# Low halves of the index key made on VectorE in place of GpSimd, in a hybrid retention and sparse-attention layer

## The chip, the cores and the metric

The kernel runs on one core of one Trainium2 chip, in one launch. The metric is the device time of that core in microseconds; lower is better. Times of "before" and "after" are medians of several executions; one further execution of each is recorded by the hardware profiler, and every duration below comes from that recorded execution.

## The reference

One decoder layer on 512 tokens of width 1024, in float32. One projection feeds two groups of heads: four heads of chunked retention, and four heads of attention over 128 keys per query that an indexer selects. The rest is an output projection, a layer norm, a SwiGLU block of 2816 hidden units and a second layer norm. What the change touches is the indexer:

```python
iq = rope(iq.reshape(B, S, IDX_HEADS, IDX_DIM), positions)      # 8 index heads of 64
ik = rope(ik[:, :, None, :], positions)[:, :, 0, :]             # one index key per token
...
logits = jax.nn.relu(jnp.einsum('bqhd,bsd->bqhs', qb, kf))
score = jnp.einsum('bqh,bqhs->bqs', wb, logits)
score = jnp.where(key_pos[None, None, :] <= pb[None, :, None], score, -jnp.inf)
_, sel = lax.top_k(score, topk)
```

## The kernel before

**Precision by halves.** TensorE's fast float32 form (`float32r`) rounds its operands, so the kernel writes a value as a high half (a cast) and a low half (value minus high half), and `mm3` (L93 to L96) makes one product out of three matmuls: high by high (L94), high by low (L95 or L96), low by high. For weights, `split` (L85 to L91) makes the high half with a ScalarE cast (L86). The low half is made either by a VectorE subtraction (L91) or, for a share of the weights, by a ScalarE copy with sign reversed (L88) and a DMA from GpSimd's queue that adds the raw weight to it in memory (L89).

**The stage around the change.** The order of instructions is written out by hand; each engine runs its own list strictly in that order. `proj_feature(c)` projects 128 output features at a time: weight number k = 2c + i goes to the accumulator `pf{c}_{i}`, with 24 matmuls of 128x512 each. There are four accumulators of that tag in PSUM, used in turn. Weights 0 to 3 and every even one have their low half from VectorE; the odd ones from 5 on have it by the DMA on GpSimd's queue. When an accumulator is finished, `rope` (L229 to L238) turns it: three VectorE multiplications (L233 to L235), which read PSUM, and one GpSimd addition (L237), which reads two SBUF tiles. Raw weights come in chunks of two on SyncE's queue into three buffers (`raw`). A buffer is free once its last low half is made; for weights made by the DMA that means once that DMA has landed.

**The index key and the logits.** `index_rope` (L251 to L299) runs beside the projection, a step at a time. It turns the index key into `ks` (L286, VectorE), then calls `halves_k` (L255). That casts the high half `kh` on ScalarE (L256) and makes the low half in two blocks of 32 partitions, 0 to 31 and 64 to 95 (L259). After each block two DMAs on GpSimd's queue copy low and high half into the neighbouring 32 partitions (L260, L261). In the profile `kh` and both low tiles are called `kk`. `logits(j)` (L406) multiplies the eight index heads of a block of 128 queries with them, two matmuls a head (L415, L416); ScalarE applies the relu (L417), VectorE adds the head up in `score` (L421 for head 0, L423 for the others). Below, "head 4" is the fifth of the eight heads of block 1, the first block that is computed. The PSUM tiles of these logits, called `lg`, are of the other tag, again four in turn. The tile before head 0 in that turn holds the turned head weights (`iwp`), so head 4 takes the tile of head 0 and can start only when L421 has read it.

**TensorE's list here:** the last matmuls of `pf3_0` (weight 6); head 0; nine matmuls of `pf3_1` (weight 7, the low half by DMA); heads 1 and 2; nine more of `pf3_1`; heads 3 and 4; the last six of `pf3_1`; heads 5 and 6; `pf4_0`, and so on.

Of the kernel before, what the change touches and what calls it, by code (L numbers as in the profile page):

```python
# [9 lines left out]
F32 = mybir.dt.float32  # L10
# [3 lines left out]
ALU = mybir.AluOpType  # L14
# [39 lines left out]
def hybrid_layer_kernel(ctx: ExitStack, tc: tile.TileContext, xT, x, pos, w0, wf, wt, wo,  # L54
                        wgu, wd, gng, lmg, lmb, lfg, lfb, ident_d, cols_d, masks_d, decay_d, out):
    nc = tc.nc
    V, A, G, T = nc.vector, nc.scalar, nc.gpsimd, nc.tensor
# [12 lines left out]
    def psu(name):  # L70
        return psp.tile([P, 512], F32, tag="u", name=name)

    def tmp(name, dt=F32):
        return tp.tile([P, 512], dt, tag="t", name=name)
# [154 lines left out]
    def rope(dst, src, ct, st, lo=0):  # L229
        t1 = tmp("rt1")  # L230
        t2 = tmp("rt2")
        n = slice(lo, S)
        V.tensor_tensor(t1[:, n], src[:, n], ct[:, n], op=ALU.mult)  # L233
        V.tensor_tensor(t2[0:64, n], src[64:128, n], st[64:128, n], op=ALU.mult)
        V.tensor_tensor(t2[64:128, n], src[0:64, n], st[0:64, n], op=ALU.mult)  # L235
        if dst is not None:
            G.tensor_tensor(dst, t1[:, n], t2[:, n], op=ALU.add)  # L237
        return t1, t2  # L238
# [6 lines left out]
    kh, kl = kk3[:, 0], (kk3[:, 1], kk3[:, 2])  # L245
# [5 lines left out]
    def index_rope():  # L251
        G.memset(kk3[:, 1:].bitcast(F32), 0.0)
        rounding = lambda: None

        def halves_k(ks):  # L255
            A.copy(kh, ks)  # L256
            for b in (0, 64):
                s, d = slice(b, b + 32), slice(b + 32, b + 64)
                G.tensor_tensor(kl[0][s], ks[s], kh[s].bitcast(F32), op=ALU.subtract)  # L259
                nc.gpsimd.dma_start(kl[1][d].bitcast(F32), kl[0][s].bitcast(F32))  # L260
                nc.gpsimd.dma_start(kh[d].bitcast(F32), kh[s].bitcast(F32))  # L261

        def halves_q(i, qs):
            A.copy(qa[:, i], qs[:, P:])
            A.copy(qb[:, i], qs[:, P:])
            G.tensor_tensor(ql[:, i], qs[:, P:], qa[:, i].bitcast(F32), op=ALU.subtract)
            if i % 2:
                n = slice(i - 1, i + 1)
                for d, s in ((qa[32:64, n], ql[0:32, n]), (qa[96:128, n], ql[64:96, n]),
                             (qb[0:32, n], ql[32:64, n]), (qb[64:96, n], ql[96:128, n])):  # L270
                    nc.gpsimd.dma_start(d.bitcast(F32), s.bitcast(F32))

        for i in range(4):
            t1, t2 = rope(None, acc0[1 + i], CI, SI, P)
            qs = tmp("qs")
            V.tensor_tensor(qs[:, P:], t1[:, P:], t2[:, P:], op=ALU.add)
            rounding()
            rounding = lambda i=i, qs=qs: halves_q(i, qs)
            yield 2.3
        rounding()  # L280
        while len(key) < 3:
            yield 1.0
        A.copy(iwr, acc0[0])
        t1, t2 = rope(None, acc0[0], CI, SI)
        ks = tmp("ks")
        V.tensor_tensor(ks, t1, t2, op=ALU.add)  # L286
        yield 1.7
        halves_k(ks)
        yield 5.5
        iwp = psu("iwp")  # L290
        for j in range(NB):
            T.transpose(iwp[:, j * P:(j + 1) * P], iwr[:, j * P:(j + 1) * P], ident)
        iw3 = iwp.rearrange("p (j c) -> p j c", c=P)
        A.activation(iw[:, 1:], iw3[:, 1:, 32:32 + IH], AF.Copy, scale=IDX_SCALE)
        o = 0
        for a, z in SPARE:
            A.copy(early_v[:, :, o:o + z - a], iw3[:, :, a:z])
            o += z - a
        yield 3.0  # L299
# [1363 lines left out]
```

## Time and profile before

| | before |
|---|---|
| three timed executions, us | 617.75, 618.26, 618.61 |
| their median, us | 618.26 |
| the profiled execution, us | 619.8 |
| its span (first to last instruction), us | 618.0 |
| mean granted TensorE clock in it | 0.99 |
| read from HBM / written | 74.52 MB / 2.10 MB |
| instructions on VectorE / ScalarE / GpSimd | 940 / 611 / 202 |

The profiled execution lasted 619.8 us, of which its span is 618.0; 1.8 us lie around it. It stands 1.5 us above the median of the timed ones. Instants below are counted from the start of that span.

How to read the rows: "PE" is TensorE's matmuls, "DVE" VectorE, "ACT" ScalarE, "POOL" GpSimd. A row of a timeline has start, length, engine, line, operation, output and inputs, and shapes; in square brackets is how long the engine sat idle before it, and what ended that. In the chain of waits each row is a start, a length and what the end of the kernel was waiting for then. A row of the table of stretches gives the length of the stretch, then busy time of PE, PE's weight load, DVE, ACT and POOL with instruction counts, then the granted TensorE clock (1.00 is full speed), the busy share of the DMA engines and the GB/s they moved. Numbers of tiles are left out in the profile: `pf` is any of `pf0_0` to `pf7_1`.

### The profile page before, as it was taken

The numbers are of one execution on the slowest core, as the hardware profiler recorded it, in microseconds if no ns is written. First come the engines' busy times: TensorE is split into PE (matmuls) and PEld (weight loads), VectorE is DVE, ScalarE is ACT, GpSimd is POOL, SyncE is SP. The second block draws the span as 40 slices with busy tenths as digits, with TensorE's granted clock in tenths as the row PEclk, the third lists the DMA queues.
The fourth block names the chain that finished last, engine by engine and source line by source line (L and its number), as shares of the span: only waits on it lengthen the run. The fifth ranks groups of instructions, "written<-read, shape, count | busy, mean of one in ns | idle before, by whom it ended". The sixth has DMA issues, their size and how long they took to land.

```text
span 618.0 us, 9195 instructions
## 1 busy us (share of the span) xinstructions
PE 605.4 (98%) x3256; PEld 521.5 (84%) x3256; DVE 517.7 (84%) x940; ACT 348.8 (56%) x611; POOL 186.1 (30%) x202
## 2 busy tenths in 40 slices
PE   8999899999999999999999999999999999999995
PEld 7988688888888787889998888888888988887884
DVE  6888667889888977889999989898898888977856
ACT  5443244435242557687657777777677785648300
POOL 0136612331148000233003535444343421214011
PEclk9999799999999999999999999999999999999998
DMA  8875643579663582499237888888978879689602
GB/s 277 250 233 147 170 154 103 141 167 229 180 137 102 211 335 72 136 245 179 87 136 186 180 207 168 194 197 177 207 150 188 183 213 220 155 227 293 199 34 102
DMA packets 48014, 110.77 MB, mean 179 GB/s; under 512 B 8880, under 2 KB 23280, under 8 KB 42464
## 3 DMA queue, kind: packets, MB, share of 16 engines
q1 hardware_dynamic: 25232, 77.02, 37.3%
q0 software_dynamic: 22432, 32.71, 31.8%
q8 instruction: 25, 0.41, 0.3%
q10 hardware_dynamic: 304, 0.46, 0.2%
q14 instruction: 21, 0.17, 0.1%
HBM read 74.52 MB, written 2.10 MB: 124 GB/s over the span
## 4 chain that ended last, share of the span: by engine, by line
PE 72%; issue 10%; DVE 6%; DMA 5%; POOL 4%; ACT 1%; SPq 1%; POOLq 0%; ACTq 0%; DVEq 0%
PE ga L919 10%; PE ga L921 5%; PE gc L919 5%; PE ga L927 5%; PE pf L96 3%; PE pf L94 3%; PE pf L95 3%; PE gc L921 3%; PE gb L919 3%; PE mx L96 2%; PE mx L94 2%; PE mx L95 2%; PE gc L927 2%; PE pt L95 2%; PE pt L94 2%
## 5 line engine op out<-in xcount | busy, mean ns | idle before, releaser
L86 ACT CAST wh<-raw 128x1024 fp32r<-128x1024 f32 x44 | 46.1, 1050 | 41.2 <-issue 17.5
L870 POOL DMA_DIRECT2D t<-t x34 | 29.2, 857 | 85.5 <-DVE t L1003 56.8
L96 PE MATMUL pf<-xh,wl 128*128 128x512 f32 x128 | 51.0, 399 | 2.3 <-DMA wl<-raw 2.3
L94 PE MATMUL pf<-xh,wh 128*128 128x512 f32 x128 | 51.1, 399 | 0.2 <-DVE rt L235 0.2
L95 PE MATMUL pf<-xl,wh 128*128 128x512 f32 x128 | 50.8, 397 | 0.0
L870 POOL DMA_DIRECT2D w<-w x34 | 39.2, 1194 | 32.9 <-DVE w L953 23.9
L91 DVE TENSOR_TENSOR wl<-raw,wh 128x1024 fp32r<-128x1024 f32 x26 | 32.0, 1236 | 18.0 <-ACT wh L86 17.9
L472 POOL TENSOR_TENSOR rs<-ve,half 128x1 f32<-128x1 f32 (+1 forms) x11 | 11.8, 1072 | 102.9 <-DVE ve L471 102.7
L94 PE MATMUL pt<-wh,xh 128*128 128x512 f32 (+1 forms) x96 | 38.5, 402 | 0.0
L95 PE MATMUL pt<-wl,xh 128*128 128x512 f32 (+1 forms) x96 | 37.0, 386 | 0.0
L96 PE MATMUL pt<-wh,xl 128*128 128x512 f32 (+1 forms) x96 | 36.7, 382 | 0.0
L89 POOL DMA_DIRECT2D wl<-raw x18 | 15.8, 876 | 55.3 <-ACT wl L88 55.3
L96 PEld LDWEIGHTS pf<-xh,wl 128*128 128x128 f32 x128 | 24.7, 193 | 8.0 <-DMA wl<-raw 2.7
L94 PEld LDWEIGHTS pf<-xh,wh 128*128 128x128 f32 x128 | 24.6, 192 | 5.2 <-issue 0.5
L95 PEld LDWEIGHTS pf<-xl,wh 128*128 128x128 f32 x128 | 24.6, 192 | 4.7
L417 ACT ACTIVATE lg<-lg 128x256 f32<-128x256 f32 (+2 forms) x24 | 10.9, 474 | 29.8 <-PE lg L416 29.7
L434 DVE MAX8 m<-score 128x8 f32<-128x256 f32 (+2 forms) x48 | 26.8, 558 | 1.1
L435 DVE MATCH_REPLACE8 score<-m,score 128x256 f32<-128x256 f32 (+2 forms) x48 | 26.0, 542 | 0.0
L89 POOL DMA_DIRECT2D slot<-hu x9 | 10.9, 1335 | 37.3 <-ACT slot L88 37.3
L96 PEld LDWEIGHTS pt<-wh,xl 128*128 128x128 f32 x96 | 18.0, 188 | 3.3
L94 PEld LDWEIGHTS pt<-wh,xh 128*128 128x128 f32 x96 | 18.1, 188 | 2.7
L95 PEld LDWEIGHTS pt<-wl,xh 128*128 128x128 f32 x96 | 18.1, 189 | 2.4
(1183 smaller groups left out, 1979.8 us busy)
## 6 DMA issues: line engine op xcount, KB each, us to landing
graw<-in_wgu_dram SPq DMA_DIRECT2D x22, 1024.0 KB, 5.3
wl<-raw POOLq DMA_DIRECT2D x18, 512.0 KB, 5.1
raw<-in_wo_dram SPq DMA_DIRECT2D x8, 1024.0 KB, 4.9
raw<-in_wf_dram SPq DMA_DIRECT2D x7, 1024.0 KB, 6.3
raw<-in_wt_dram SPq DMA_DIRECT2D x6, 1024.0 KB, 5.3
r<-in_wd_dram SPq DMA_DIRECT2D x12, 512.0 KB, 5.8
w<-w POOLq DMA_DIRECT2D x34, 128.0 KB, 4.1
graw<-graw POOLq DMA_DIRECT2D x17, 256.0 KB, 3.7
```

The lines of the kernel that those rows point to most:

```text
L86: A.copy(hi, src)
L89: nc.gpsimd.dma_start(lo.bitcast(F32), src, accum_op=ALU.add)
L91: eng_lo.tensor_tensor(lo, src, hi.bitcast(F32), op=ALU.subtract)
L94: T.matmul(acc, lhsT=lh, rhs=rh, start=first, stop=False, **kw)
L95: T.matmul(acc, lhsT=lh, rhs=rl, start=False, stop=False, **kw)
L96: T.matmul(acc, lhsT=ll, rhs=rh, start=False, stop=last, **kw)
L434: V.max(m8, a)
L435: V.match_replace(out=a, in_to_replace=m8, in_values=a, imm_value=TAKEN)
L870: nc.gpsimd.dma_start(t[:, :Q], t[:, Q:], accum_op=ALU.add)
L919: T.matmul(pair, lhsT=h[:, ws[k]], rhs=parts[q][:, :, k], start=first and k == 0, stop=False, skip_group_check=True)
L921: T.matmul(full[:, :Q], lhsT=l[:, ws[k]], rhs=parts[q][:, 0, k], start=False, stop=k == 3, skip_group_check=True)
L927: T.matmul(gp[n][acc], lhsT=a[:, i * S + k * P:i * S + k * P + P], rhs=parts[q][:, b, k], start=first and j == 0, stop=j == 11, skip_group ...
```

## The change

The subtraction that makes the two blocks of the key's low half is issued on VectorE in place of GpSimd. Nothing else differs: the same operands, shapes and place in the program's text.

```diff
             A.copy(kh, ks)
             for b in (0, 64):
                 s, d = slice(b, b + 32), slice(b + 32, b + 64)
-                G.tensor_tensor(kl[0][s], ks[s], kh[s].bitcast(F32), op=ALU.subtract)
+                V.tensor_tensor(kl[0][s], ks[s], kh[s].bitcast(F32), op=ALU.subtract)
                 nc.gpsimd.dma_start(kl[1][d].bitcast(F32), kl[0][s].bitcast(F32))
                 nc.gpsimd.dma_start(kh[d].bitcast(F32), kh[s].bitcast(F32))
```

On GpSimd this is the piece where it happens, between the addition of `pf1_0`'s rope and the DMA that finishes the low half of weight 7 (`wl_592`); the semaphores that each row waits for are in brackets (DMASW: an earlier DMA of GpSimd's queue, Pool: GpSimd itself).

```order
 L237 TENSOR_TENSOR akT<-rt_557,rt_558 128x512 [waits DVE_49]
-L259 TENSOR_TENSOR kk_301<-ks,kk_301 32x512 [waits Activation_49]
-L260 DMA kk_301<-kk_301 32x512 [waits DMASW4_49,Pool_49]
-L261 DMA kk_301<-kk_301 32x512 [waits DMASW5_49]
-L259 TENSOR_TENSOR kk_301<-ks,kk_301 32x512
-L260 DMA kk_301<-kk_301 32x512 [waits DMASW6_49,Pool_49]
+L260 DMA kk_301<-kk_301 32x512 [waits DMASW4_49,DVE_49]
+L261 DMA kk_301<-kk_301 32x512 [waits DMASW5_49,Activation_49]
+L260 DMA kk_301<-kk_301 32x512 [waits DMASW6_49,DVE_49]
 L261 DMA kk_301<-kk_301 32x512 [waits DMASW7_49]
 L89 DMA wl_592<-raw_358 128x1024 [waits DMAHW1_49,DMASW0_49,Activation_49]
```

GpSimd keeps its four DMAs and loses two additions of 32x512; its first and third DMA now wait for VectorE instead of for itself.

On VectorE the two subtractions land between the rope multiplications of `pf1_0` (`rt_558`) and those of `pf1_1` (`rt_600`).

```order
 L234 TENSOR_TENSOR rt_558<-pf_0_497,tables 64x512
 L235 TENSOR_TENSOR rt_558<-pf_0_497,tables 64x512
+L259 TENSOR_TENSOR kk_301<-ks,kk_301 32x512 [waits Activation_49]
+L259 TENSOR_TENSOR kk_301<-ks,kk_301 32x512
 L233 TENSOR_TENSOR rt_600<-pf_1_553,tables 128x512 [waits PE_49,Pool_49]
 L234 TENSOR_TENSOR rt_601<-pf_1_553,tables 64x512
```

All that follows on VectorE stands behind them now. That is first the rope of `pf1_1`, the low half of weight 8, the ropes of `pf2_0` and `pf2_1`, and then these rows, up to the one that reads head 0's logits (`lg_0_708`); they are the same rows in both kernels:

```order
L91 TENSOR_TENSOR wl_715<-raw_547,wh_714 128x1024
L233 TENSOR_TENSOR rt_722<-pf_0_677,tables 128x512
L234 TENSOR_TENSOR rt_723<-pf_0_677,tables 64x512
L235 TENSOR_TENSOR rt_723<-pf_0_677,tables 64x512
L421 TENSOR_SCALAR score<-lg_0_708,iw 128x256
```

TensorE's list is unchanged. Its piece with heads 3 and 4, where the wait for VectorE (DVE) is the one for the tile of head 0:

```order
L415 MATMUL lg_3_753<-kk_301,qb 128x256 [waits PE_49,Activation_49]
L416 MATMUL lg_3_753<-kk_301,qb 128x256
L415 MATMUL lg_4_758<-kk_301,qa 128x256 [waits DMASW1_49,DVE_49]
L416 MATMUL lg_4_758<-kk_301,qa 128x256
L94 MATMUL pf_1_718<-xh_76,wh_591 128x512
```

Nothing moved in it; only the instants at which what it waits for is ready can differ.

## The prediction

> **What bounds the kernel now.** I read the page first: who is busy, and what the end waited for.
>
> ```profile
> span 618.0 us, 9195 instructions
> PE 605.4 (98%) x3256; PEld 521.5 (84%) x3256; DVE 517.7 (84%) x940; ACT 348.8 (56%) x611; POOL 186.1 (30%) x202
> PE 72%; issue 10%; DVE 6%; DMA 5%; POOL 4%; ACT 1%; SPq 1%; POOLq 0%; ACTq 0%; DVEq 0%
> ```
>
> TensorE is busy nearly all the time. So what shortens this kernel is a wait of TensorE, or a stretch in which it runs slowly. The view of TensorE's waits has one wait of size in the middle of the kernel:
>
> ```profile
> PE pf L96 <- DMA wl<-raw: 2.3, 1, 2.3
> ```
>
> TensorE's timeline shows where, and what follows. Third row from the top: `pf3_1` begins, and two rows later it lacks the low half of weight 7.
>
> ```profile
> 66.90 0.39 PE L96 MATMUL pf<-xh,wl 128*128 128x512 f32 x1
> 67.42 0.36 PE L415 MATMUL lg<-kk,qa 128*128 128x256 f32 x1
> ...
> 67.74 0.40 PE L94 MATMUL pf<-xh,wh 128*128 128x512 f32 x1
> 67.97 0.39 PE L95 MATMUL pf<-xl,wh 128*128 128x512 f32 x1
> 70.66 0.80 PE L96 MATMUL pf<-xh,wl 128*128 128x512 f32 x1 [2.29 <-DMA wl<-raw]
> ...
> 77.75 0.28 PE L415 MATMUL lg<-kk,qb 128*128 128x256 f32 x1
> ...
> 77.97 0.28 PE L415 MATMUL lg<-kk,qa 128*128 128x256 f32 x1
> ```
>
> A full matmul starts 0.23 us after the one before (67.74 to 67.97), a head of block 1 takes 0.22 (77.75 to 77.97). From head 0 (67.42) to head 4 (77.97) lie 18 matmuls and four heads: 18 x 0.23 + 4 x 0.22 = 5.02 us at that pace. It took 10.55. The wait explains 2.29; the table of stretches has the rest in its clock column:
>
> ```profile
> 6.50:8.50 2.00, 1.16 (x7) 0.84 (x6) 1.25 (x2) 1.64 (x3) 0.00 (x0) 1.00 0.99 306
> ...
> 68.40:70.00 1.60, 0.00 (x0) 0.00 (x0) 0.71 (x1) 0.85 (x1) 1.60 (x2) 1.00 1.08 205
> 70.70:76.50 5.80, 5.80 (x16) 4.74 (x17) 3.31 (x6) 0.74 (x2) 2.30 (x2) 0.50 1.02 266
> 77.00:80.00 3.00, 3.00 (x18) 2.58 (x18) 0.97 (x2) 0.65 (x2) 0.00 (x0) 1.00 0.72 300
> ...
> 610.60:612.50 1.90, 0.03 (x1) 0.00 (x0) 1.79 (x5) 0.30 (x1) 0.00 (x0) 1.00 0.43 161
> 613.00:618.00 5.00, 0.00 (x0) 0.00 (x0) 1.73 (x4) 0.00 (x0) 0.00 (x0) 0.50 0.28 105
> ```
>
> After 1.6 us of idleness the granted clock halves, and it stays there until about 77. From 70.66 to 77.97 stand 16 matmuls and three heads, 4.34 us at full pace; they took 7.31, so the slow clock cost **2.97**. The idle 0.84 us between 6.5 and 8.5 (1.16 busy of 2.00) cost no clock; the idleness at the end did, after 1.9 us.
>
> Why was the low half late? The chain of waits runs back from it through GpSimd, one thing behind the other:
>
> ```profile
> 59.51 1.29 POOL akT L237
> 60.80 1.25 POOL kk L259
> ...
> 62.33 0.48 POOL kk L260
> ...
> 62.82 0.51 POOL kk L261
> ...
> 63.40 1.30 POOL kk L259
> ...
> 64.99 0.46 POOL kk L260
> ...
> 65.48 0.50 POOL kk L261
> 65.98 4.63 DMA wl<-raw
> ```
>
> The data of that DMA were there long before; here is ScalarE, then the times to landing of the `kk` DMAs and of the `wl` DMAs around here:
>
> ```profile
> 57.79 1.06 ACT L88 ACTIVATE wl<-raw 128x1024 fp32r<-128x1024 f32 x1
> ```
>
> ```profile
> DMA to landing us min/median/max: 1.8/1.9/1.9
> ```
>
> ```profile
> DMA to landing us min/median/max: 4.5/4.6/5.3
> ```
>
> So the two subtractions on GpSimd stand in a chain that ends at TensorE. They hold up head 0 a little too: the last `kk` DMA, issued at 65.48, lands at about 67.4, where head 0 starts; without that it would start at 66.90 + 0.23 = 67.13.
>
> **The change part by part.** *GpSimd* loses two operations of 1.25 and 1.30 us and the two pauses of 0.28 behind them (62.05 to 62.33, 64.70 to 64.99). The four `kk` DMAs, about 0.5 us each, could follow the addition that ends at 60.80; the `wl` DMA would be issued at 62.8 instead of 65.98 and land at 67.4 (with 5.3 at 68.1). TensorE asks for it at 67.13 + 0.22 + 2 x 0.23 = 67.81. The wait of 2.29 shrinks to 0 to 0.3, below the 0.84 that cost no clock. SyncE's next raw load, which needs this landing, starts earlier as well.
>
> *VectorE* gains the two subtractions. Their cover is an idle piece further down its list:
>
> ```profile
> 55.59 0.69 DVE L286 TENSOR_TENSOR ks<-rt,rt 128x512 f32<-128x512 f32 x1
> 56.20 1.22 DVE L91 TENSOR_TENSOR wl<-raw,wh 128x1024 fp32r<-128x1024 f32 x1
> ...
> 58.74 0.69 DVE L235 TENSOR_TENSOR rt<-pf,tables 64x512 f32<-64x512 f32 x1
> 59.45 0.69 DVE L233 TENSOR_TENSOR rt<-pf,tables 128x512 f32<-128x512 f32 x1
> ...
> 69.29 1.30 DVE L91 TENSOR_TENSOR wl<-raw,wh 128x1024 fp32r<-128x1024 f32 x1 [2.03 <-ACT wh L86]
> ...
> 72.62 0.48 DVE L421 TENSOR_SCALAR score<-lg,iw 128x256 f32<-128x256 f32 x1
> ```
>
> Nearest is L286, 512 elements from two SBUF tiles: the next row starts 0.61 later. Two are 1.22, from 59.45 on; their input, the cast `kh`, was ready at 56.9:
>
> ```profile
> L256 ACT CAST kk<-ks x1: 620/620/620, 56.3 to 56.3; 128x512 fp32r<-128x512 f32 x1
> ```
>
> All that follows on VectorE comes 1.22 later, until the idle 2.03 before 69.29. That waits for a ScalarE cast behind head 0's relu, which comes 0.29 earlier; 1.74 of idleness is left, enough. Then L421 comes 0.29 earlier, ending at 72.62 + 0.48 - 0.29 = 72.81.
>
> *What is late next.* TensorE, at full pace from 67.13, reaches head 4 at 72.15. Head 4 needs the tile that L421 reads. With 0.08 from an end to the start it releases (58.74 + 0.69 to 59.51), it starts at 72.9: a new wait of 0.75, which did not show while TensorE was late itself. Gain: 77.97 - 72.9 = **5.07**.
>
> *The unknown.* The subtractions stand right beside GpSimd's addition of 59.51, and the trace shows what a VectorE operation on two SBUF tiles does beside one:
>
> ```profile
> L427 DVE TENSOR_TENSOR score<-score,masks x3: 293/1057/1161, 84.0 to 116.5; 128x128 f32<-128x128 f32 x3
> ```
>
> ```profile
> 83.44 1.60 POOL L237 TENSOR_TENSOR aqT<-rt,rt 128x512 f32<-128x512 f32 x1
> ```
>
> L427 takes 0.29 alone and 1.16 at 84.04, ending where GpSimd's addition ends: it is blocked. So the other end: both subtractions run after 60.80, until 62.02, and VectorE is 2.57 late, 0.83 more than the idle piece covers. L421 ends at 73.64, head 4 starts at 73.72, gain 77.97 - 73.72 = **4.25**. The `kk` DMAs then wait for the first subtraction (61.4), the `wl` DMA goes out at 63.5 and lands at 68.1 to 68.8, 0.3 to 1.0 after it is asked for. That costs nothing more, because it comes out of the 1.57 us that TensorE waits at head 4 anyway. I take the blocked case, 4.25, since L427 is the nearest row.
>
> The Trainium skill speaks against this change here: "SBUF — State Buffer", "Who interferes with whom", says that a VectorE instruction with two SBUF inputs contends with a GpSimd instruction that reads SBUF, and that the loser is blocked for the whole instruction. L427's 0.29 against 1.16 agrees; by that rule the gain is 4.25, without it 5.07.
>
> Behind head 4, TensorE has hardly a wait to the end (the page's 98%), its loads are released by its own progress, and so I carry the gain to the end whole. The profiled execution lies 1.5 us above the median, and I apply the difference to the median: 618.26 - 4.25 = **614.0**.
>
> **The rivals.** *No slow clock in the timed executions.* The phase of the clock's fall may differ between executions. Without it head 4 was at 75.0 before (77.97 - 2.97), and the gain is 75.0 - 73.72 = 1.3 to 75.0 - 72.9 = 2.1: **616.2 to 617.0**. For it speaks that the profiled execution is 1.5 longer than the median; against it that it did fall, twice in this trace, both times within 2 us. "TensorE: Matmul & The Clock Gate" in the Trainium skill ("What's actually happening") has the clock fall after an idle window of about 3.4 us; by that rule a wait of 2.29 need not halve it, but this trace shows 0.50 behind such a wait.
>
> *VectorE becomes the bound.* The low halves of weights 8 and 10 (L91) also read two SBUF tiles, in front of L421, and GpSimd's additions, now earlier, may block them: 0.87 each (1.16 - 0.29). L421 then ends at 75.4, TensorE waits 3.2 at head 4, the clock falls there and costs 2.97. That is 0.5 slower, **618.8**; with one more such block 1.3 slower, **619.6**. It decides from an end of L421 at 75.0 on. Against it: before, with the same neighbours, the second of these took 1.30, hardly over the 1.22 of 56.20.
>
> *Nothing arrives at the end.* If the landing were set by something else than its issue, or a later stage gave the time back: **618.3**. Against it stand the chain, and that the DMA took 4.63, its usual time.
>
> **How the numbers follow.** Forecast 0.74 (613.2 to 614.6), no slow clock 0.13, VectorE the bound 0.09, nothing 0.04. The range from 612.8 to 617.0 takes in the first two and leaves out some 0.17. A measurement can tell 0.2%, 1.24 us, from no change. Faster by more: the forecast, nearly all of the second, a little of the third, 0.87; the rest of the small cases, 0.08, within; 0.05 slower.
>
> **What would show it.** Right: `wl` issued on GpSimd by 63.5, no TensorE wait over 1 us at L96, a clock of 1.00 from 68 to 77, head 4 at about 73.7, just behind L421. The subtractions end at 62.0 if blocked, at 60.7 if not. Wrong: a fallen clock behind head 4, L421 later than 75, or the gain at 80 us missing at the end.

## The result, and the profile after

| | before | after |
|---|---|---|
| timed executions, median, us | 618.26 (617.38 to 618.89, 5 runs) | 614.25 (613.73 to 615.65, 5 runs) |
| ratio of the times, with 95% interval | | 0.9941 [0.9925, 0.9957] |
| profiled execution / its span, us | 619.8 / 618.0 | 614.24 / 612.4 |

The changed kernel is faster by 0.6%, between 2.7 and 4.6 us by the interval. The forecast was 614.0. The ratios here and below leave out executions in a slower state of the chip; there was one, of e1_fill (697 us, at a mean granted clock of 0.81).

The views are read in the same order as before. First TensorE's waits of the changed kernel (engine, line, what it waited for, us in all, times, longest):

```profile
PE warm L191 <- DVE cold L188: 1.2, 1, 1.2
PE lg L415 <- DVE score L421: 0.7, 1, 0.7
PE ri L528 <- DVE rst L502: 0.3, 1, 0.3
```

The 2.3 us for the low half of weight 7 are gone. In their place is a wait of 0.7 for L421, VectorE's row that releases the tile of head 0. TensorE's timeline has both places:

```profile
66.32 0.28 PE L415 MATMUL lg<-kk,qa 128*128 128x256 f32 x1
...
66.78 0.40 PE L95 MATMUL pf<-xl,wh 128*128 128x512 f32 x1
67.12 0.50 PE L96 MATMUL pf<-xh,wl 128*128 128x512 f32 x1
...
72.42 0.39 PE L415 MATMUL lg<-kk,qa 128*128 128x256 f32 x1 [0.67 <-DVE score L421]
```

L96, the first matmul with the late low half, starts 0.34 after the one ahead of it, 0.11 more than the usual 0.23. Head 0 to head 4 takes 6.10 us in place of 10.55. GpSimd's timeline shows why:

```profile
58.74 1.78 POOL L237 TENSOR_TENSOR akT<-rt,rt 128x512 f32<-128x512 f32 x1 [3.68 <-DVE rt L235]
60.47 0.51 POOL L260 DMA_DIRECT2D kk<-kk  x1
60.96 0.51 POOL L261 DMA_DIRECT2D kk<-kk  x1
61.47 0.50 POOL L260 DMA_DIRECT2D kk<-kk  x1
61.96 0.50 POOL L261 DMA_DIRECT2D kk<-kk  x1
62.45 0.95 POOL L89 DMA_DIRECT2D wl<-raw  x1
63.28 2.33 POOL L237 TENSOR_TENSOR akT<-rt,rt 128x512 f32<-128x512 f32 x1
```

The weight's DMA goes out 3.71 us behind the start of that addition (62.45 - 58.74); before it was 6.47 (65.98 - 59.51). VectorE's timeline, with the two subtractions in one merged row, shows the price:

```profile
57.97 0.68 DVE L235 TENSOR_TENSOR rt<-pf,tables 64x512 f32<-64x512 f32 x1
58.69 2.38 DVE L259 TENSOR_TENSOR kk<-ks,kk 32x512 fp32r<-32x512 f32 x2
61.10 0.69 DVE L233 TENSOR_TENSOR rt<-pf,tables 128x512 f32<-128x512 f32 x1
...
63.23 1.23 DVE L91 TENSOR_TENSOR wl<-raw,wh 128x1024 fp32r<-128x1024 f32 x1
...
68.62 1.23 DVE L91 TENSOR_TENSOR wl<-raw,wh 128x1024 fp32r<-128x1024 f32 x1
...
71.88 0.48 DVE L421 TENSOR_SCALAR score<-lg,iw 128x256 f32<-128x256 f32 x1
```

The pair of subtractions took 2.38, where e4_early below shows 1.39 with nothing beside it, and GpSimd's addition took 1.78 in place of 1.29: both lost. The view of that line has the shortest, the middle and the longest time of the two, in ns:

```profile
L259 DVE TENSOR_TENSOR kk<-ks,kk x2: 680/1176/1671, 58.7 to 59.4; 32x512 fp32r<-32x512 f32 x2
```

The first subtraction began 0.05 ahead of the addition and took 0.68, unhindered; the addition was held up by it, and the second subtraction, 1.67, by the addition. All of this ran at full clock (PEclk, the third column from the end):

```profile
68.00:70.00 2.00, 2.00 (x13) 1.70 (x11) 1.97 (x3) 0.72 (x3) 1.97 (x2) 1.00 0.74 246
70.00:72.00 2.00, 1.75 (x9) 1.31 (x7) 1.94 (x4) 0.15 (x1) 1.07 (x2) 1.00 0.92 264
72.00:74.00 2.00, 1.58 (x8) 1.36 (x9) 1.66 (x4) 0.59 (x2) 1.21 (x1) 1.00 1.10 229
```

To compare profiles, take one stretch: from L286, which turns the index key and is the same in all kernels, to the first matmul of the token projection (`pt1_0`). In the changed kernel these two rows are:

```profile
54.82 0.69 DVE L286 TENSOR_TENSOR ks<-rt,rt 128x512 f32<-128x512 f32 x1
```

```profile
125.03 0.36 PE L94 MATMUL pt<-wh,xh 128*128 128x456 f32 x1
```

That is 70.21 us. Before, the second row stood at 130.46 and the first at 55.59: 74.87. So 4.66 of the 5.6 us between the two spans arose here. The remaining 0.9 lies outside, where the kernels are alike; over all profiles of the two kernels what lies outside the stretch varies from 542.1 to 543.4.

### The profile page after: what moved, and what is told of

It is laid out like the page before. It is cut to its first block, busy times and chain, and to the rows that moved or that the text cites. A ratio compares the mean times of both kernels' runs of the same rounds, so it can differ in the third digit from the quotient of the medians.

```text
span 612.4 us, 9196 instructions
## 1 busy us (share of the span) xinstructions
PE 602.6 (98%) x3256; PEld 520.1 (85%) x3256; DVE 519.7 (85%) x942; ACT 348.8 (57%) x611; POOL 186.0 (30%) x200
## 4 chain that ended last, share of the span: by engine, by line
PE 90%; DVE 5%; issue 3%; POOL 1%; ACT 0%; POOLq 0%; DVEq 0%
PE ga L919 10%; PE ga L921 5%; PE gc L919 5%; PE ga L927 5%; PE pf L94 5%; PE pf L95 5%; PE pf L96 5%; PE acc L218 3%; PE gc L921 3%; PE gb L919 3%; PE mx L96 2%; PE mx L94 2%; PE dl L96 2%; PE mx L95 2%; PE dl L95 2%
## 5 line engine op out<-in xcount | busy, mean ns | idle before, releaser
L96 PE MATMUL pf<-xh,wl 128*128 128x512 f32 x128 | 50.0, 391 | 0.0
L91 DVE TENSOR_TENSOR wl<-raw,wh 128x1024 fp32r<-128x1024 f32 x26 | 31.6, 1221 | 15.9 <-ACT wh L86 15.8
L96 PE MATMUL pt<-wh,xl 128*128 128x512 f32 (+1 forms) x96 | 36.7, 382 | 0.0
L96 PEld LDWEIGHTS pf<-xh,wl 128*128 128x128 f32 x128 | 24.0, 188 | 5.5 <-DMA wl<-raw 0.4
L96 PEld LDWEIGHTS pt<-wh,xl 128*128 128x128 f32 x96 | 18.0, 188 | 3.3
L1003 DVE TENSOR_TENSOR t<-t,gc 128x512 f32<-128x512 f32 x17 | 11.7, 687 | 10.1 <-ACT t L1002 10.1
```

What stands on the lines that cost most here:

```text
L91: eng_lo.tensor_tensor(lo, src, hi.bitcast(F32), op=ALU.subtract)
L96: T.matmul(acc, lhsT=ll, rhs=rh, start=False, stop=last, **kw)
```

## The experiments

Ten further runs followed, each (but the two profiles e7) timed in five rounds against the kernel before on the same chip. The theory: the late DMA of weight 7 made TensorE wait and lowered its clock; the change moved it forward, and what remains is VectorE's list in front of head 4. Rivals: the key's halves being ready early, or the quicker engine, made the gain; and, within the theory, that the clock's part does not arise in the timed executions.

| kernel | ratio to before, 95% interval | stretch, us | TensorE's wait there, us | clock behind it |
|---|---|---|---|---|
| before, three profiles | | 74.87, 72.09, 73.62 | 2.3, 2.3, 2.3 at L96 | 0.50 long, 1.00, 0.50 short |
| after | 0.9941 [0.9925, 0.9957] | 70.21 | 0.7 at head 4 | 1.00 |
| e8_after (the same) | 0.9952 [0.9938, 0.9965] | 70.21 | 0.6 at head 4 | 1.00 |
| e1_fill | 0.9982 [0.9972, 0.9992] | 72.05 | filled | full pace |
| e2_pad | 1.0011 [0.9996, 1.0025] | 75.00 | 2.9 at L96 | 0.50 |
| e3_one | 1.0003 [0.9991, 1.0015] | 71.92 | 2.3 at L96 | 1.00 |
| e4_early | 0.9963 [0.9950, 0.9976] | 70.42 | 1.1 at head 4 | 1.00 |
| e5_dmafirst | 1.0027 [1.0011, 1.0042] | 75.81 | 4.1 at head 0 | 0.50 |
| e6_first | 0.9952 [0.9937, 0.9968] | 70.15 | 0.2 at head 5 | 1.00 |
| e8_both | 0.9937 [0.9922, 0.9952] | 69.19 | none listed | 1.00 |

**e2_pad: give GpSimd its delay back, and nothing else.**

```diff
                 nc.gpsimd.dma_start(kh[d].bitcast(F32), kh[s].bitcast(F32))
+            for b in (0, 64):
+                G.tensor_tensor(ks[b:b + 32], ks[b:b + 32], ks[b:b + 32], op=ALU.add)
```

> The changed kernel, with two additions of 32x512 on GpSimd (on the index key tile, which nothing reads afterwards) between the key's four DMAs and the DMA of weight 7's low half. The low halves stay on VectorE and the key's DMAs go out as early as in the changed kernel. Theory (what counts is when GpSimd reaches the DMA of weight 7): issued 2.5 us later, landing at about 69.6, TensorE waits 2.3 to 2.6 us at L96, the clock halves, time 617.5 to 618.5. Rival (the gain came from the key's halves being ready early, or from VectorE being the quicker engine for the subtraction): 614.3, as the changed kernel.

The gain is gone: 1.0011. The key's DMAs went out early, 60.86 to 62.84, and head 0 did not wait. But the weight's DMA was behind the two additions, and TensorE waited for it, 2.9 in place of the 2.3 to 2.6 expected, because the two additions took 3.04. GpSimd's timeline, then TensorE's waits:

```profile
62.34 0.50 POOL L261 DMA_DIRECT2D kk<-kk  x1
62.85 3.04 POOL L263 TENSOR_TENSOR ks<-ks 32x512 f32<-32x512 f32 x2
65.85 0.91 POOL L89 DMA_DIRECT2D wl<-raw  x1
```

```profile
PE pf L96 <- DMA wl<-raw: 2.9, 1, 2.9
```

So neither the early key nor VectorE as the quicker engine makes the gain. The instant at which GpSimd reaches that DMA does: the additions also delay what stands behind it on GpSimd, but the DMA is what TensorE waited for.

**e1_fill: keep the wait, take the idleness out of it.**

```diff
             acc = psd(f"pf{c}_{i}")
...
+            if c == 3 and i == 1:
+                for _ in range(10):
+                    T.matmul(acc, lhsT=cold[:, :P], rhs=cold, start=True, stop=True)
```

> The kernel before, with ten extra matmuls of 128x512 in bfloat16 on TensorE ahead of pf3_1; their results go to the accumulator of pf3_1 and are overwritten by its first matmul. Nothing on GpSimd or VectorE changes, so the low half of weight 7 lands as late as before. Theory (the late low half costs 2.29 us of waiting and, through the halved clock, 2.97 more, in the timed executions too): the wait of 2.29 is filled, the clock stays at 1.00 from 68 to 77 us, head 0 to head 4 takes about 7.6 us in place of 10.55, and the time is 618.26 - 2.97 = 615.3. Rival (the clock does not fall in the timed executions): 618.3, no change.

The fillers ran from 67.21 on, L96 started at 70.13, and the matmuls behind it came every 0.23 us (in this profile the clock column reads a flat 0.95 throughout, so the pace is the evidence). The ratio, 0.9982 [0.9972, 0.9992], is a gain of 0.5 to 1.7 us on 618.26, not of 2.97. So the slow clock costs something in the timed executions, but on average less than it did in the one profile that the prediction was made from. The next two profiles say why.

**e7_before_a and e7_before_b: the kernel before, profiled again.** No edit.

> The kernel before, unchanged, profiled again. The wait at L96 should be 2.3 us again. If the fall of the clock depends on where the wait lies in a fixed rhythm of the clock's monitor, the clock column behind the wait differs between executions: 0.50 in some, 1.00 in others (as behind the 2.26 us wait of e3_one), and the span by up to 2.97. If it hangs on the length of the wait alone: 0.50 again, and a span within 1 us of 618.0.

> The same again, for a third profile of the kernel before: with two or more clocks to compare, 0.50 in all of them speaks for the length of the wait, a mixture for the rhythm.

They took 616.0 and 618.66, with spans of 614.2 and 616.9. Both waited 2.3 at L96 like the first profile. The table of stretches of the first, behind its wait, which ends at 70.08:

```profile
67.80:70.00 2.20, 0.00 (x0) 0.00 (x0) 1.29 (x2) 0.87 (x1) 2.20 (x3) 1.00 0.79 149
70.10:77.00 6.90, 6.90 (x36) 5.91 (x37) 4.29 (x8) 1.63 (x6) 2.34 (x2) 1.00 1.01 286
```

and of the second, whose wait ends at 70.25:

```profile
70.30:70.80 0.50, 0.50 (x2) 0.44 (x3) 0.49 (x2) 0.00 (x0) 0.50 (x1) 0.95 0.72 139
70.90:74.10 3.20, 3.20 (x11) 2.74 (x10) 1.77 (x4) 0.37 (x1) 1.70 (x2) 0.50 1.03 189
74.20:77.00 2.80, 2.80 (x15) 2.36 (x15) 0.88 (x3) 0.71 (x3) 0.00 (x0) 1.00 1.01 424
```

The same kernel, the same wait, and three outcomes: no fall, a short one, and a long one in the first profile (from 70.0 to about 76.8). The length of the wait alone does not decide it; where the wait lies in a rhythm of the clock does, as the last section works out. The stretches differ accordingly: 72.09, 73.62 (1.5 more) and 74.87 (2.8 more), on average 1.4 of clock, in line with e1_fill's 0.5 to 1.7. The fall also accounts for much of the spread of the times before (615.85 to 619.0 in the 29 executions beside e1 to e4): of all 57 executions of the kernel before that ran beside the experiments, the 39 with a mean granted clock of 0.990 to 0.995 average 618.2, the 18 with 0.996 to 0.998 average 616.9.

**e3_one: move one block only.**

```diff
-                G.tensor_tensor(kl[0][s], ks[s], kh[s].bitcast(F32), op=ALU.subtract)
+                (G if b else V).tensor_tensor(kl[0][s], ks[s], kh[s].bitcast(F32), op=ALU.subtract)
```

> The kernel before with only the first of the two blocks subtracted on VectorE, the second on GpSimd. Theory: GpSimd reaches the DMA of weight 7 at about 64.1 (on the changed kernel's time axis, where it was 62.45), TensorE waits about 1.7 us at L96 instead of 0.1, VectorE is earlier so that the wait at head 4 is gone. If the clock holds through such a wait, head 4 comes 1.0 later than in the changed kernel: 615.2. If the clock halves as before: up to 2.97 more, 618.2. Rival (the gain goes by halves moved, not by waits): the middle, 616.3.

Nothing is gained, 1.0003, and the estimate of 64.1 for the DMA was off by about 1 us. Before, it went out 6.47 behind the start of GpSimd's addition; here 6.33 (66.48 - 60.15):

```profile
60.15 1.78 POOL L237 TENSOR_TENSOR akT<-rt,rt 128x512 f32<-128x512 f32 x1 [3.69 <-DVE rt L235]
...
62.96 2.23 POOL L259 TENSOR_TENSOR kk<-ks,kk 32x512 fp32r<-32x512 f32 x1
...
66.48 0.95 POOL L89 DMA_DIRECT2D wl<-raw  x1
```

VectorE's one subtraction is this row:

```profile
60.10 0.68 DVE L259 TENSOR_TENSOR kk<-ks,kk 32x512 fp32r<-32x512 f32 x1
```

It is not blocked, and the addition beside it still takes 1.78: the first subtraction of the pair is what slows that addition. The subtraction left on GpSimd takes 2.23 in place of 1.29, because it now meets VectorE's L91 for weight 8 (62.82 to 64.05). That is not "the middle" of the rival, and it shows that the blocking works in both directions. The clock held behind this wait of 2.26, a further case for the mixture above.

**e5_dmafirst: leave the work on GpSimd, change its order.**

```diff
             A.copy(kh, ks)
+            pending.append(lambda: halves_low(ks))
+
+        def halves_low(ks):
             for b in (0, 64):
```

> The kernel before, both subtractions still on GpSimd, but the key's low halves and their four DMAs stand behind the DMA of weight 7's low half instead of ahead of it. Theory (what counts is what stands ahead of TensorE's next need on GpSimd): weight 7 is issued at about 60.8, 5 us earlier, and L96 does not wait; the last DMA of the key lands at about 68.8 or, if VectorE blocks a GpSimd subtraction as in e3_one, up to 1.5 later, so the wait moves to head 0 and is 1.7 to 3.2 us. Time between 616 and 618, near the kernel before: the two users of GpSimd's time cannot both be early. Rival (only the weight's DMA matters): the whole gain without VectorE, 614 to 615.

L96 does not wait any more, but head 0 waits 4.1 us for the key, more than the 1.7 to 3.2 expected, and the kernel is slower than before, 1.0027. The key's last DMA was issued at 66.81; the four `kk` DMAs took up to 5.2 us to land, where 1.9 was usual:

```profile
DMA to landing us min/median/max: 2.2/3.6/5.2
```

I put that down to the raw load, which starts when weight 7 lands and now ran beside them. The trace agrees: that load began at 65.81, the two `kk` DMAs issued ahead of it (63.60, 64.13) landed within 2.2 to 2.5, the two behind it (66.32, 66.81) took 4.8 to 5.2. No run tested it by itself. In both orders of GpSimd's list that ran, either the weight or the key is late; of the kernels here, both are early only where GpSimd has neither the subtractions nor other work in their place.

**e4_early: the subtractions away from GpSimd's addition.**

```diff
         V.tensor_tensor(ks, t1, t2, op=ALU.add)
+        pending.append(lambda: halves_k(ks))
         yield 1.7
-        halves_k(ks)
```

> The changed kernel with the key's halves (cast, two subtractions, four DMAs) called one step earlier: on VectorE behind the low half of weight 6 and ahead of the rope of pf1_0, on GpSimd ahead of the addition of that rope, when GpSimd is idle. Theory (the subtractions are blocked by GpSimd's addition, and the 0.67 us wait of TensorE at head 4 is what that delay leaves): the two subtractions take 1.2 to 1.3 us in place of 2.38, L421 ends about 1 us earlier, the wait at head 4 is 0 to 0.1, time 614.25 - 0.6 = 613.6. Rival (the subtraction takes 1.2 us each whatever runs beside it): 2.4 again, the rope of pf1_0 ends late, pf3_0 waits about 0.9 us for its accumulator, time 614.3 to 615.2.

`pending` is a list of pieces that are issued a step later; here it puts the key's halves ahead of the rope of `pf1_0`. The first half of the theory holds: with GpSimd idle the pair takes 1.39 in place of 2.38. The second does not: the wait at head 4 became 1.1, and the stretch 70.42, no better. The row blocked now is another one, the low half of weight 10. GpSimd's timeline, then VectorE's:

```profile
68.00 1.30 POOL L237 TENSOR_TENSOR aqT<-rt,rt 128x512 f32<-128x512 f32 x1
```

```profile
56.88 1.39 DVE L259 TENSOR_TENSOR kk<-ks,kk 32x512 fp32r<-32x512 f32 x2
...
68.46 1.93 DVE L91 TENSOR_TENSOR wl<-raw,wh 128x1024 fp32r<-128x1024 f32 x1 [0.55 <-ACT wh L86]
```

GpSimd's addition began first, at 68.00, and L91 took 1.93 in place of 1.23. VectorE had also stood idle 0.55 ahead of it, waiting for ScalarE's cast, so that about half of what the pair saved was gone before. In the changed kernel it is the other way round: L91 begins at 68.62, the addition at 68.67, and the addition takes 2.33 while L91 keeps 1.23.

**e6_first: take L421 out from behind that row.**

```diff
                 A.activation(lp[:, :n], lp[:, :n], AF.Relu)
-            if h >= 1:
+            if j == 1 and h == 0:
+                V.tensor_scalar(acc[:, :n], lp[:, :n], iw[:, j, 0:1], 0.0, op0=ALU.mult, op1=ALU.add)
+            if h >= (2 if j == 1 else 1):
```

> The changed kernel with one VectorE row moved: head 0 of block 1 is scaled into the score (L421, here L419) as soon as its relu is done, ahead of the low half of weight 10 and the rope of pf3_0. Theory (the 0.67 us wait of TensorE at head 4 hangs on that row's place in VectorE's list): the row ends near 68 in place of 72.4, the wait at head 4 is gone, 614.25 - 0.67 = 613.6; the later heads' rows come as late as before and nobody waits for them. Rival (the next head's tile is late in its place): a wait of about 0.5 at head 5, 614.2.

Head 4 does not wait, but here the rival was nearer: L91 is blocked (2.03), heads 5 and 6 wait about 0.25 each, and the stretch is 70.15, the same as after. The ratio, 0.9952, is no better either.

**e8_both and e8_after: both edits, beside the changed kernel.** The diff is that of e4_early and e6_first together; e8_after has none.

> The changed kernel with both edits of e4_early and e6_first: the key's halves ahead of the rope of pf1_0, and head 0's score row ahead of the low half of weight 10. Theory (in this stretch VectorE's list is as long as TensorE's, so a wait that one edit removes comes back behind the next blocked row; the two edits together give VectorE about 1 us of room): no wait of TensorE over 0.2 us at heads 4 to 6, 0.4 to 0.7 below the changed kernel of the same call, the stretch from the start of L286 to the first matmul of pt1_0 69.6 to 69.8 us in place of 70.21. Rival (VectorE stays the pace through the block of weight 10's low half): no difference to the changed kernel, 70.2.

> The changed kernel again, unchanged, beside the one above on the same chip and against the same executions of the kernel before: 0.990 to 0.996 of the time before, as at first; in its profile no wait of TensorE over 1 us at L96 and a clock of 1.00 from 64 to 80, since a wait of 0.7 leaves the clock alone wherever it lies.

No wait of TensorE is listed in the stretch any more, which takes 69.19, 1.02 less than after; I had expected 0.4 to 0.7. The medians of the two, timed side by side, are 613.63 (613.43 to 614.66) against 614.84 (614.18 to 615.36) for the changed kernel; the intervals of the ratios still overlap, so that e8_both beats the changed kernel is clear in the profile and only likely in the times. Against the kernel before it is clear, 0.9937.

## Why the prediction was right, and where a size was off

**The chain from GpSimd to TensorE** held as put: the DMA of weight 7 went out early, L96 waited 0.1, and e2_pad, which delays that DMA again and leaves the key early, takes the whole gain away.

**The blocked case** was the right end to take, but by a picture that was half right. The subtractions ended at 61.07, which on the time axis of before (0.77 later) is 61.84; 62.02 was said for blocked, 60.7 for not. The prediction had both of them behind GpSimd's addition. In fact the first ran ahead of it (0.68) and delayed it by 0.49 (1.78 - 1.29), and only the second was blocked (1.67). One subtraction less behind the addition and an addition that ends 0.49 later nearly cancel, so that the instant came out within 0.2 is in part luck. The rule of the Trainium skill behind it ("SBUF — State Buffer", "Who interferes with whom") adds that the order of issue decides who is blocked; L91 at 68.62 ahead of an addition at 68.67, and at 68.46 behind one at 68.00, agree with it, and so do the two subtractions.

**What is late next** was named rightly, L421 and head 4. Its size was off: a wait of 1.57 was said, less what a late weight would take of it, and 0.67 was found. L421 ended 14.39 behind the start of L235 (72.36 - 57.97), where the sum had 14.90 (73.64 - 58.74). The 0.5 lie in three places: the pair ended a little sooner (61.84 in place of 62.02), and the two L91 behind it took 1.23 where the sum kept the 1.55 and 1.30 of before. The first of those, 1.55, had run beside GpSimd's first subtraction (60.76 to 62.03), which the change takes away. I had counted the block that the change makes, and not the one that it takes away.

**The slow clock** is the term that was mis-sized. The prediction carried 2.97 us of it from one profile to the median, and kept "no slow clock" as a rival of all or nothing. It is a matter of each execution: 2.8, 1.5 and 0 in three profiles, about 1.1 by e1_fill. (A reading behind it was a little off too: at the end of the trace the clock was still full after 1.9 us of idleness and fell at 612.73, 2.1 us behind the last matmul.) With the gain of the wait alone, 72.09 - 70.21 = 1.9, an average of 1.1 to 1.4 makes 3.0 to 3.3 in the timed executions. The first timing has 3.6 (0.9941), the repeat e8_after 3.0 (0.9952), and both intervals hold that sum. The profile pair's 4.66 is the case of a full fall. So the 614.0 came out of two errors of opposite sign: L421 earlier by 0.5, the clock taken 1.5 to 1.9 dearer than it is on average (2.97 less 1.4 of the three profiles, or less 1.1 of e1_fill). They do not cancel wholly. That the forecast lies 0.25 from the measured 614.25 is luck: a median 0.7 to 1.0 higher would fit the mechanism better, and the repeat had 614.84.

**VectorE as the bound**, the rival with a slower end, did not come, but its mechanism is real: L91 of weight 10 was blocked in e4_early, e6_first and e8_both, 0.7 to 0.8 each, where 0.87 was the price said. It needs the addition to begin first.

## What to carry to other kernels

Work on an engine that is idle most of the time can still bound the kernel, if a transfer that the busy engine needs stands behind it in the same list; look at the order there, not at the share of busy time. When an operation is moved beside another, count both the collision that it makes and the one that it takes away, and expect a wait that one edit removes to come back behind the next blocked row, as in e4_early and e6_first, until the list has room. A cost that hangs on the clock has to be read from several profiles of the same kernel before it goes into a sum.

## What the hardware showed that I had not expected

The same 2.3 us wait of TensorE lowered the clock in two of three profiles of one kernel, for 6.8 us in one and 3.4 in another, and not at all in the third. The traces say why. The clock changes on a fixed rhythm with a step of 3.413 us. In the first profile it falls at 70.01, rises at 76.84 and falls for good, behind the last matmul, at 612.73: 2 steps and 157 steps. In e7_before_b the instants are 70.75, 74.16 and 613.47 (1 and 158 steps), in e2_pad 69.66, 76.49 and 612.38 (2 and 157), in e5_dmafirst 69.98, 76.81 and 616.11 (2 and 158). Where the clock did not fall behind the wait, the steps can be counted back from the fall at the end (611.49 in e7_before_a, 612.11 in e3_one). What then counts is how long TensorE idles within one step:

| run | step that holds most of the wait | idle in it, us | clock behind it |
|---|---|---|---|
| e7_before_a | 68.77 to 72.19 (the step before it has 1.14) | 1.31 | 1.00 |
| e3_one | 69.39 to 72.81 | 1.76 | 1.00 |
| before | 66.60 to 70.01 | 1.79 | 0.50 |
| e2_pad | 66.25 to 69.66 | 2.08 | 0.50 |
| e7_before_b | 67.34 to 70.75 | 2.30 | 0.50 |
| e5_dmafirst | 66.57 to 69.98 | 2.38 | 0.50 |

Over all steps at full clock in all twelve profiles, those with 1.79 of idleness or more ended in a fall and those with 1.76 or less did not (idle as the profile counts it, whose ends of matmuls are modelled). Where the rest of the wait reached into the next step (0.64 in before, 0.81 in e2_pad, 1.75 in e5_dmafirst) the clock stayed low for one step more; where none did (e7_before_b), it rose after one. "TensorE: Matmul & The Clock Gate" in the Trainium skill ("What's actually happening") describes such a free-running window.

An estimate from these numbers: if a wait of 2.3 lies anywhere in the rhythm with equal chance, a boundary splits it into two parts that are both too short in 37% of the executions (no fall), the fall lasts one step in 48% (1.5 us) and two in 15% (2.8 us). That is 1.1 us on average, what e1_fill measured. The waits of 0.6 to 1.1 at head 4 are too short to lower the clock wherever they lie, and did not in three profiles.

In these runs an elementwise operation costs the same on 32 partitions as on 128: GpSimd's subtraction of 32x512 took 1.27 and 1.29, its addition of 128x512 1.29; VectorE's pair of 32x512 took 1.39 undisturbed, twice L286's 0.69.
